# The experts dealt to the fourteen blocks of a mixture anew, and one one-hot written a quarter earlier

## The chip, the cores and the metric

The kernel runs on one core of a Trainium2 chip. A core has a matrix engine (TensorE; PE in the profile, with PEld for the loading of its stationary operand), three engines for elementwise work (VectorE, DVE; ScalarE, ACT; GpSimd, POOL), and SyncE (SP), which issues the loads from the chip's memory here. The metric is the device time of one execution in microseconds (us): the median of several runs, lower is better.

## The reference

A two-layer encoder over 512 tokens of width 1024. Each layer adds a mixer (windowed attention beside a short convolution, and one output projection) and then a mixture of experts to the stream; a final norm ends it. The change touches the mixture alone:

```python
group_logits = (xf @ w_rg).astype(jnp.float32) + b_rg.astype(jnp.float32)
grp = jnp.argmax(group_logits, axis=-1)              # one of 4 groups
...
top_logit, top_local = lax.top_k(in_group, TOP_K)    # 2 of its 8 experts
gates = p_grp * jax.nn.softmax(top_logit, axis=-1)
...
def expert_block(args):
    xb, e = args
    return (jax.nn.silu(xb @ w_gate[e]) * (xb @ w_up[e])) @ w_down[e]
```

Each of the 512 tokens goes to two of 32 experts. An expert has w_gate and w_up of 1024 x 512 and w_down of 512 x 1024, all float32: 6.3 MB, and all 32 of them are read in each layer.

## The kernel before

**Slots and blocks.** The router ranks the experts of a layer by how many tokens they got. The ranks below STATIC (0 to 3) are given to experts 0 to 3 whatever their counts, so that their weights can be loaded before the router has decided; the others go by size, rank 4 the largest. The table BLOCKS (lines 39 to 54) is fixed when the kernel is built: a block is 128 rows of TensorE's output, and its entries (rank, slots) say which ranks share the rows and how many slots each gets. The slots of a rank, 128, 96, 64 or 32, are the same wherever it stands. RANK, BASE, SLOTS, OFF and FIRST are worked out from the table, and the routing (order, route) takes its constants from them. What does not fit goes through spill, a loop that runs as often as the counts need.

**One block**, function block(b, between). Gate and up: in four quarters (kq) of the 1024 inputs, first gate and then up, for each expert of the block two matmul calls per piece of rows into the PSUM buffers "A". A piece is as wide as the smallest step that fits the block's slots (w in the code: 128, 64 or 32 rows), and the pieces of a block stand side by side in the array. Then Silu on ACT and a product on DVE, four transposes ("B"), and down in four quarters c into "C"; last, the result is split into a high and a low part (yhi, ylo) for the sum. The functions in `between` run after quarter 0, 1, 2 or 3 of gate and up, or at "a" and "t" between gate/up and down.

**What runs in between.** For the next group of blocks (GROUPS pairs them: (0,1), (2), (3,4), (5,6), ...): onehot(j) writes the 0/1 matrix of tokens by slots, eight DVE instructions on a 128 x 256 tile each and one small one on POOL; rows_of and slots look up each slot's token and gate; gather multiplies the tokens by the one-hot into the block's inputs. For the block before: combine adds its result into x, with a PSUM pair "D", "F" and an add on DVE for each half of a tile (line 1282). In block 2 all_parts splits the stream x into a high part (ACT, line 1175) and a low part (DVE, line 1176) once for all later gathers; the gathers before that use x itself. SUMS lets block 4 add two blocks' results and block 5 two more.

**Loads.** load() lists every weight tile in the order of use (the list todo): for each block by quarter, gate before up, expert by expert, and then the down tiles. A tile is 512 KB. An expert has twelve: four gate, four up, four down. pump() issues the next loads on SP's queue as long as fewer than N4 - keep tiles are held (N4 = 42 buffers in the pool t4); done() gives a tile back after its last matmul and pumps again. The rest of the pool serves hidden inputs, one-hots, the parts of x and the blocks' results; mem["keep"] is set by stage (20 for blocks 3 and 4, then 15, and 21 in the last block but one). SP runs its loads in the order of the program, and each waits there until the buffer that it was given is free. The weights of ranks 4 and up are fetched with the expert's number in a register, so only after order().

**Order of the engines.** In the blocks TensorE's instructions are kept in program order (pin(T)), each behind the instruction before it on its engine. The instructions of DVE, ACT and POOL are placed by a planner at build time. At block 8 a register is loaded on all engines (the count for spill) between two blocks.

Of the kernel before, what the change touches and what calls it, by code (L numbers as in the profile page):

```python
# [40 lines left out]
    [(2, 64), (3, 64)],  # L41
    [(19, 32), (20, 32), (21, 32), (22, 32)],
    [(8, 64), (9, 64)],
    [(4, 128)],
    [(10, 64), (11, 64)],
    [(5, 96), (23, 32)],
    [(12, 64), (13, 64)],
    [(6, 96), (24, 32)],
    [(14, 64), (15, 64)],
    [(7, 96), (25, 32)],  # L50
    [(18, 64), (26, 32), (27, 32)],
    [(28, 32), (29, 32), (30, 32), (31, 32)],
    [(16, 64), (17, 64)],
]
NBLK = len(BLOCKS)
RANK, BASE, SLOTS, OFF, FIRST = [], [], [], [], []
# [122 lines left out]
def trunk(ctx, tc, x_d, norm_mix, w_in, attn_sink, conv_w, norm_attn_out, norm_conv_out, w_out,  # L179
# [10 lines left out]
    def t4(shape, dt=F32):  # L190
        return t4p.tile(list(shape), dt, name="t4", tag="t4")

    def t2(shape, dt=F32):
        return t2p.tile(list(shape), dt, name="t2", tag="t2")

    def ps(tag, shape=(P, 512)):
        return psp.tile(list(shape), F32, name=tag, tag=tag, bufs=1 if tag in "DF" else 2)

    def small(name, shape, dt=F32, bufs=1):
        return smp.tile(list(shape), dt, name=name, tag=name, bufs=bufs)  # L200

    def f(ap):
        return ap.bitcast(F32)
# [138 lines left out]
    def pin(*engines):  # L342
        for e in (V, A, T, GP):
            e.pinned = e in engines
# [655 lines left out]
    def past(q):  # L1000

        ab, sc = q["ab"], q["sc"]

        cn = ps("B", (P, 4))
        a0 = _cols["rank"][0]
        for t in range(NT):
            T.matmul(cn[:E, 0:1], ab[:, t], onesb[:, 0:1], start=t == 0, stop=t == NT - 1)
        T.matmul(cn[:E, 1:2], q["mt"], cst[:E, a0 + 2:a0 + 3], start=True, stop=True)
        V.tensor_copy(sc[:, 3:4], cn[:E, 1:2])
        V.tensor_tensor(sc[:, 2:3], cn[:E, 0:1], sc[:, 3:4], op=OP.subtract)  # L1010
        V.tensor_scalar(sc[:, 5:6], sc[:, 2:3], 0.0, None, op0=OP.is_gt)
        for b in range(1, 4):
            V.tensor_scalar(sc[:, 6:7], sc[:, 2:3], float(P * b), None, op0=OP.is_gt)
            V.tensor_tensor(sc[:, 5:6], sc[:, 5:6], sc[:, 6:7], op=OP.add)
        nbb = t2([E, P])
        V.tensor_copy(nbb, sc[:, 5:6].to_broadcast([E, P]))
        return nbb

    def places(q, nbb):

        v, oh1, oh2, wk = (q[n] for n in ("v", "oh1", "oh2", "wk"))

        def col(n):
            return v[:, n, :]

        bp = ps("B", (P, E + 1))
        T.matmul(bp, nbb, C("below")[:E], start=True, stop=True)
        bs = small("bs", [P, E + 1])
        V.tensor_copy(bs, bp)

        rb_ = small("rowso", [P, E])
        V.scalar_tensor_tensor(rb_, bs[:, :E], float(P), q["rows"][:, 0], op0=OP.mult, op1=OP.subtract)
        V.tensor_scalar(rb_, rb_, 1.0, None, op0=OP.add)
        ov = q["me"]
        V.tensor_tensor(ov, q["rks"], rb_[:, None, :].to_broadcast([P, NT, E]), op=OP.add)
        V.tensor_tensor(ov, ov, q["ge"], op=OP.mult)
        for n, oh in ((0, oh1), (1, oh2)):
            V.tensor_tensor(wk, oh, ov, op=OP.mult)
            V.tensor_reduce(col(20 + n), wk, axis=AX.X, op=OP.add)
            V.tensor_scalar(col(20 + n), col(20 + n), -1.0, None, op0=OP.add)  # L1040

        eb = t4([1, MAXB, E])
        V.tensor_tensor(eb, bs[0:1, None, 1:E + 1].to_broadcast([1, MAXB, E]),
                        iota[0:1, :MAXB, None].to_broadcast([1, MAXB, E]), op=OP.is_le)
        et = small("et", [1, MAXB])
        V.tensor_reduce(et, eb, axis=AX.X, op=OP.add)
        V.tensor_scalar(et, et, float(E - 1), None, op0=OP.min)
        ni = small("ni", [1, 4], I32)
        V.tensor_copy(ni[:, 0:1], bs[0:1, E:E + 1])
        return et, ni  # L1050
# [89 lines left out]
    def moe(l, before):  # L1140
# [4 lines left out]
        def onehot(j):  # L1145

            b, w = GROUPS[j][0], len(GROUPS[j]) * P
            sq = small("sq", [P, 2, NT], bufs=2)
            GP.tensor_scalar(sq, q["v"][:, 16:18, :], -float(b * P), None, op0=OP.add)  # L1149
            oh = t4([P, NT, 2 * P], F32R)  # L1150
            io = iota[:, :w]
            for t in range(NT):
                V.tensor_scalar(oh[:, t, :w], io, sq[:, 0, t:t + 1], None, op0=OP.is_equal)
                V.scalar_tensor_tensor(oh[:, t, :w], io, sq[:, 1, t:t + 1], f(oh[:, t, :w]), op0=OP.is_equal, op1=OP.add)  # L1154
            ohq[j] = oh
# [51 lines left out]
        def rows_of(j):  # L1207
            w = len(GROUPS[j]) * P
            p = ps("B", (P, 2 * P))
            for t in range(NT):  # L1210
                T.matmul(p[:NROW, :w], st["tab"][:, t], ohq[j][:, t, :w], start=t == 0, stop=t == NT - 1)
            st["rows"] = t2([NROW, 2 * P])
            A.activation(st["rows"][:, :w], p[:NROW, :w], AF.Copy)
# [61 lines left out]
        def combine(b, t, tags="DF"):  # L1275
            yhi, ylo, gm = yy[b]
            for n in range(2):
                s = slice(n * 512, (n + 1) * 512)
                p = ps(tags[n])
                T.matmul(p, gm[:, t * P:(t + 1) * P], yhi[:, s], start=True, stop=False)  # L1280
                T.matmul(p, gm[:, t * P:(t + 1) * P], ylo[:, s], start=False, stop=True)
                V.tensor_add(x[:, t, s], x[:, t, s], p)  # L1282
# [3 lines left out]
        def begin(t):  # L1286

            sums[t] = [ps(tag) for tag in BANKS[l][t]]
            for n in range(2):
                T.matmul(sums[t][n], ident, x[:, t, n * 512:(n + 1) * 512], start=True, stop=False)  # L1290
# [32 lines left out]
        def both(*what):  # L1323
            return lambda: [fn() for fn in what]
# [6 lines left out]
        for b in range(NBLK):  # L1331
            if b == 5:
                nbb = past(q)
            if b == 6:
                et, ni = places(q, nbb)
            if b == 8:
                over = et, nc.values_load(
                    ni[0:1, 0:1], min_val=0, max_val=MAXB,
                    skip_runtime_bounds_check_because="an expert's slots are 32 at least: fewer blocks than experts")

            late = SUMS.get(b, [b - 1])
            c = [lambda t=t: [combine(n, t) for n in late] for t in range(NT)]
            j = GROUP_OF[b] + 1
            if b == 0:
                mem["experts"] = True
                btw = {0: lambda: order(l, q), 1: rest, 3: first, "a": lambda: gather1(1, 4, ND)}
            elif b == 1:
                mem["keep"] = KEEP_SECOND
                btw = {1: lambda: onehot(1), "a": both(lambda: rows_of(1), lambda: gather1(2, 0, 4)),
                       "t": both(lambda: slots(1), lambda: gather1(2, 4, ND))}  # L1350
            elif b == 2:
                ga = [lambda k=k: gather(j, k) for k in range(0, ND, 2)]
                btw = {1: lambda: onehot(j), 2: all_parts, "a": both(lambda: rows_of(j), ga[0], ga[1]),
                       "t": both(ga[2], lambda: slots(j), ga[3])}
            elif b == NBLK - 1:
                mem["keep"] = KEEP_MOE
                btw = {0: both(c[0], c[1]), 1: both(c[2], c[3]), "a": lambda: spill(l, q, *over),
                       "t": lambda: [begin(t) for t in range(AHEAD[l])]}
                if not overflow:
                    del btw["a"]  # L1360
            elif b % 2:
                mem["keep"] = KEEP_LATE if b == 3 else KEEP_MOE
                ga = [lambda k=k: gather(j, k) for k in (0, 2)]
                btw = {1: lambda: onehot(j), "a": both(c[0], ga[0], c[1]), "t": both(c[2], ga[1], c[3])}
            else:
                ga = [lambda k=k: gather(j, k) for k in (4, 6)]
                btw = {"a": both(lambda: rows_of(j), c[0], ga[0], c[1]), "t": both(c[2], lambda: slots(j), ga[1], c[3])}
            pin(*((T,) if b < PIN_MOE else ()))
            if b == NBLK - 2:
                mem["keep"] = KEEP_MOE + 6  # L1370
            block(b, btw)
# [9 lines left out]
    for l in range(DEPTH):  # L1381
        before = moe(l, before)
# [44 lines left out]
```

## Time and profile before

| | us |
|---|---|
| median of 3 runs | 1406.32 (1406.25 to 1407.89) |
| the profiled execution | 1408.32 |
| its span, first to last instruction | 1406.5 |
| PE busy in the span | 1340.6 (95%) |
| PEld busy | 774.8 (55%) |
| DVE busy | 608.9 (43%) |
| ACT busy | 374.0 (27%) |
| POOL busy | 118.8 (8%) |

TensorE's granted clock is 0.993 of full speed over the span. The loads move 439.61 MB, 313 GB/s on the mean. Lines with L175 are those of a helper through which the engines' calls go, so the tile names say what an instruction is: A gate and up, C down, B gathers and transposes, D and F the adds of a block's result. Experts run in layer 0 from about 231 to 704 us and in layer 1 from about 924 to 1400 us. A matmul on float32 shows as two rows, and the matmuls of pieces that stand side by side overlap. Loads are counted from 1 within a layer where the text numbers them, blocks from 0.

### The profile page before, as it was taken

How to read it: one execution, taken by the hardware profiler on the slowest of the kernel's cores; microseconds unless marked ns; L12 is line 12 of the kernel's file. 1: busy time of each engine (PE TensorE's matmuls, PEld its weight loads, DVE VectorE, ACT ScalarE, POOL GpSimd, SP SyncE). 2: the span in 40 equal slices, each digit the busy share in tenths (PEclk: the TensorE clock that was granted, in tenths of full speed). 3: DMA queues.
4: the chain of work that ended last, by engine and by line, in shares of the span. 5: the costliest groups of instructions: out<-in, count | busy, mean ns of one | idle time of the engine just before them, and what ended most of it. 6: DMA issues, size and time to landing. Idle time of an engine off the chain costs nothing. (4 is left out here: it accounts for less than half of the span.)

```text
span 1406.5 us, 21931 instructions
## 1 busy us (share of the span) xinstructions
PE 1340.6 (95%) x7783; PEld 774.8 (55%) x7783; DVE 608.9 (43%) x1483; ACT 374.0 (27%) x816; POOL 118.8 (8%) x130
## 2 busy tenths in 40 slices
PE   5999999999999999999989999999899999999997
PEld 5888786545544444433368887864445444454143
DVE  4788845222344322322267888341333443324032
ACT  4556631221101111101155656221211011111002
POOL 2101440000000000000030015200000000000000
PEclk9999999999999999999999999999999999999999
DMA  8521368999989999999971224789999899999995
GB/s 266 169 74 62 114 247 305 348 378 418 403 329 357 418 413 419 419 418 420 361 240 45 76 75 136 263 335 352 397 419 363 314 418 409 418 419 419 419 419 229
DMA packets 161106, 439.61 MB, mean 313 GB/s; under 512 B 19368, under 2 KB 56416, under 8 KB 160992
## 3 DMA queue, kind: packets, MB, share of 16 engines
q1 hardware_dynamic: 160992, 438.16, 80.6%
q8 instruction: 63, 1.03, 0.3%
q14 instruction: 51, 0.42, 0.1%
HBM read 436.00 MB, written 2.10 MB: 311 GB/s over the span
## 5 line engine op out<-in xcount | busy, mean ns | idle before, releaser
L175 PE MATMUL A<-t,t 128*32 128x512 f32 (+3 forms) x3724 | 720.7, 527 | 13.9 <-DMA t<-in_w_expert_up_dram 4.0
L175 PEld LDWEIGHTS A<-t,t 128*32 128x32 f32 (+2 forms) x3724 | 343.5, 145 | 344.2 <-issue 240.0
L175 PE MATMUL C<-t,t 128*32 128x512 f32 (+4 forms) x1384 | 232.1, 567 | 3.0 <-ACT t L1256 1.5
L175 PEld LDWEIGHTS C<-t,t 128*32 128x32 f32 (+2 forms) x1384 | 84.5, 128 | 134.8 <-issue 112.9
L396 DVE SCALAR_TENSOR_TENSOR t<-C,tg,t 128x512 fp32r<-128x512 f32 x56 | 41.5, 749 | 204.4 <-ACT t L395 202.6
L175 PE MATMUL B<-t,t 128*128 128x256 f32 (+3 forms) x836 | 115.0, 289 | 7.4 <-DVE t L1176 4.9
L175 PEld LDWEIGHTS B<-t,t 128*128 128x128 f32 (+1 forms) x836 | 106.7, 191 | 23.1 <-DVE t L1176 7.8
L1251 DVE SCALAR_TENSOR_TENSOR t<-A,tg,t 128x512 f32<-128x512 f32 x28 | 21.0, 750 | 222.3 <-PE A L175 206.4
L175 PE MATMUL D<-t,t 128*128 128x512 f32 (+1 forms) x374 | 99.7, 365 | 9.9 <-DVE x L1282 6.4
L1282 DVE TENSOR_TENSOR x<-x,D 128x512 f32<-128x512 f32 x104 | 71.3, 685 | 83.9 <-PE D L175 83.5
L1250 ACT ACTIVATE t<-A,tg 128x512 f32<-128x512 f32 x28 | 19.2, 687 | 311.2 <-PE A L175 289.3
L395 ACT ACTIVATE t<-C,tg 128x512 fp32r<-128x512 f32 x56 | 37.8, 687 | 205.5 <-PE C L175 205.2
L175 POOL TENSOR_TENSOR t<-t,t 128x512 f32<-128x512 f32 (+1 forms) x34 | 63.8, 1881 | 236.2 <-PE A L175 124.3
L175 PE MATMUL B<-cst,t 128*128 128x128 f32 (+1 forms) x396 | 61.6, 284 | 21.7 <-DVE t L175 18.0
L1191 ACT ACTIVATE t<-B,gf 128x256 f32<-128x256 f32 (+1 forms) x96 | 38.3, 454 | 146.2 <-PE B L175 136.5
L175 PEld LDWEIGHTS D<-t,t 128*128 128x128 f32 x374 | 53.3, 177 | 40.6 <-issue 13.2
L1282 DVE TENSOR_TENSOR x<-x,F 128x512 f32<-128x512 f32 x104 | 70.8, 680 | 7.5 <-PE F L175 7.5
L175 PE MATMUL F<-t,t 128*128 128x512 f32 x214 | 72.0, 416 | 0.2
L175 PEld LDWEIGHTS B<-cst,t 128*128 128x128 f32 (+1 forms) x396 | 50.4, 154 | 34.7 <-issue 12.7
L175 PEld LDWEIGHTS F<-t,t 128*128 128x128 f32 x214 | 36.7, 188 | 23.1 <-DVE x L1282 14.2
L392 ACT ACTIVATE t<-t 128x1024 fp32r<-128x1024 f32 x44 | 46.1, 1058 | 0.2
L1149 POOL TENSOR_SCALAR sq<-rv 128x8 f32<-128x8 f32 x16 | 3.9, 248 | 492.0 <-DVE t L1154 456.9
(250 smaller groups left out, 1033.4 us busy)
## 6 DMA issues: line engine op xcount, KB each, us to landing
t<-in_w_expert_gate_dram SPq DMA_DIRECT2D x256, 512.0 KB, 9.8
t<-in_w_expert_up_dram SPq DMA_DIRECT2D x256, 512.0 KB, 9.3
t<-in_w_expert_down_dram SPq DMA_DIRECT2D x256, 512.0 KB, 9.8
t<-in_w_in_dram SPq DMA_DIRECT2D x36, 512.0 KB, 6.1
t<-in_w_out_dram SPq DMA_DIRECT2D x16, 512.0 KB, 3.8
x<-in_x_dram SPq DMA_DIRECT2D x4, 512.0 KB
out_dram<-t SPq DMA_DIRECT2D x3, 512.0 KB, 2.6
t<-in_norm_mix_dram SPq DMA_DIRECT2D x2, 512.0 KB
```

The costliest lines, as they stand in the source:

```text
L175: return (lambda *args, **kw: self.tc.keep_in_program_order(fn(*args, **kw))) if self.pinned else fn
L392: A.activation(hi, src, AF.Copy)
L395: A.activation(hi, src, AF.Copy, scale=scale)
L396: V.scalar_tensor_tensor(lo, src, scale, f(hi), op0=OP.mult, op1=OP.subtract)
L1149: GP.tensor_scalar(sq, q["v"][:, 16:18, :], -float(b * P), None, op0=OP.add)
L1191: A.activation(hg[b][c // 4][:, c % 4 + cc, :w], p[:, cc, :w], AF.Copy, scale=g_ffn[:, c + cc:c + cc + 1])
L1250: A.activation(a, pg, AF.Silu, scale=rs)
L1251: V.scalar_tensor_tensor(a, pu, rs, a, op0=OP.mult, op1=OP.mult)
L1282: V.tensor_add(x[:, t, s], x[:, t, s], p)
```

## The change

The table keeps every rank and its slots and deals them to the blocks anew from the block numbered 4 on. Before, the blocks held 2, 2, 4, 2, 1, 2, 2, 2, 2, 2, 2, 3, 4 and 2 experts; after, 2, 2, 4, 2, 2, 3, 2, 3, 1, 2, 2, 2, 2 and 3. The one block with a single expert (rank 4, 128 slots) is the ninth instead of the fifth, and there is one four-expert block, the third, instead of two. Since the list of loads follows the table, the weights come in the new order. Of the fourteen blocks seven instead of six have pieces of 32 rows, and six instead of seven pieces of 64.

The second part moves onehot(j) of the third block (b == 2), which writes the one-hot for blocks 3 and 4, from behind the second quarter of gate and up to behind the first.

```diff
     [(2, 64), (3, 64)],
     [(19, 32), (20, 32), (21, 32), (22, 32)],
     [(8, 64), (9, 64)],
+    [(5, 96), (29, 32)],
+    [(16, 64), (23, 32), (24, 32)],
+    [(10, 64), (11, 64)],
+    [(17, 64), (25, 32), (26, 32)],
     [(4, 128)],
-    [(10, 64), (11, 64)],
-    [(5, 96), (23, 32)],
+    [(6, 96), (30, 32)],
     [(12, 64), (13, 64)],
-    [(6, 96), (24, 32)],
+    [(7, 96), (31, 32)],
     [(14, 64), (15, 64)],
-    [(7, 96), (25, 32)],
-    [(18, 64), (26, 32), (27, 32)],
-    [(28, 32), (29, 32), (30, 32), (31, 32)],
-    [(16, 64), (17, 64)],
+    [(18, 64), (27, 32), (28, 32)],
 ]
...
             elif b == 2:
                 ga = [lambda k=k: gather(j, k) for k in range(0, ND, 2)]
-                btw = {1: lambda: onehot(j), 2: all_parts, "a": both(lambda: rows_of(j), ga[0], ga[1]),
+                btw = {0: lambda: onehot(j), 2: all_parts, "a": both(lambda: rows_of(j), ga[0], ga[1]),
                        "t": both(ga[2], lambda: slots(j), ga[3])}
```

## The prediction, made before the changed kernel ran

> **What bounds the kernel now.** I read the page's slices first, then the timeline of TensorE's own row (PE) through one layer's experts, then the busy time by stretch, one stretch per block, and last the queue of SP.
>
> ```profile
> span 1406.5 us, 21931 instructions
> ...
> DMA  8521368999989999999971224789999899999995
> ```
>
> The two runs of 9 are the two layers' experts: the transfers are full there, and PE looks full too. The PE timeline at block 12 of layer 0, of four experts, shows which one is late. Columns: start, length, then the instructions; what ended an idle gap stands in brackets.
>
> ```profile
> 613.70 6.87 PE L175 MATMUL A<-t,t 128*32 128x512 f32 x50
> 620.75 1.04 PE L175 MATMUL A<-t,t 128*32 128x512 f32 x2 [0.19 <-DMA t<-in_w_expert_up_dram]
> ...
> 643.57 1.90 PE L175 MATMUL A<-t,t 128*32 128x512 f32 x10 [0.19 <-DMA t<-in_w_expert_up_dram]
> ...
> 654.08 4.49 PE L175 MATMUL C<-t,t 128*32 128x512 f32 x38
> ...
> 663.78 1.90 PE L175 MATMUL C<-t,t 128*32 128x512 f32 x10 [0.25 <-DMA t<-in_w_expert_down_dram]
> 665.62 2.94 PE L175 MATMUL A<-t,t 128*64 128x512 f32 x10
> ...
> 670.64 0.73 PE L175 MATMUL D<-t,t 128*128 128x512 f32 x2
> ...
> 692.38 7.09 PE L175 MATMUL C<-t,t 128*64 128x512 f32 x32
> ```
>
> A is gate and up, C is down. Elsewhere the same work takes this long, whatever the widths of the slots:
>
> ```profile
> 330.61 13.96 PE L175 MATMUL A<-t,t 128*64 128x512 f32 x64
> ...
> 359.97 14.00 PE L175 MATMUL A<-t,t 128*128 128x512 f32 x32
> ...
> 432.85 13.94 PE L175 MATMUL A<-t,t 128*32 128x512 f32 x128
> ...
> 456.04 7.07 PE L175 MATMUL C<-t,t 128*32 128x512 f32 x64
> ```
>
> So block 12's A took 613.70 to 645.47, 31.8 us for 13.9: 17.8 lost. Its C took 654.08 to 665.68, 11.6 for 7.1: 4.5 lost. The next block's first quarter took 665.62 to 670.64, 5.0 for a quarter of 13.96 (3.5) and a change of work: 1.4 lost. Together **23.7 us in a layer wait for weights**, though each bracket is small. PE is "busy" there because matmuls that wait between loads count as long rows.
>
> The stretches say why. The columns are PE, PEld, DVE, ACT, POOL busy, PE's granted clock, the transfers' share, GB/s.
>
> ```profile
> 360.00:396.30 36.30, 35.15 (x127) 19.45 (x126) 13.80 (x27) 4.72 (x9) 0.00 (x0) 1.00 0.92 366
> 396.30:432.50 36.20, 34.80 (x171) 16.42 (x170) 16.66 (x38) 3.54 (x7) 0.23 (x1) 1.00 0.84 310
> 432.50:463.00 30.50, 30.50 (x256) 14.29 (x254) 12.81 (x33) 5.26 (x10) 0.00 (x0) 1.00 1.03 418
> 463.00:498.60 35.60, 35.60 (x192) 14.76 (x188) 10.71 (x21) 4.37 (x9) 0.23 (x1) 1.00 1.03 414
> 613.70:665.60 51.90, 47.52 (x254) 15.23 (x246) 7.91 (x16) 4.76 (x10) 0.00 (x0) 1.00 1.03 419
> ```
>
> 419 GB/s is the queue at full pace: a load of 512 KB (524,288 bytes) takes 1.25 us, an expert (12 loads) 15.0. A block of two experts is 30.0 us of queue beside about 30 us of PE, as 432.50:463.00 shows: a balance. Block 4 has one expert, 15 us of queue beside 36.3 of PE. The buffers fill, and the queue stands still: (419 - 366)/419 x 36.3 = 4.6 us in this stretch, (419 - 310)/419 x 36.2 = 9.4 in the next, **14.0 together**. That time is missing at the four-expert block, which asks for 60 us of queue at once. Layer 1 repeats it:
>
> ```profile
> 1053.00:1089.50 36.50, 35.36 (x131) 19.62 (x130) 14.03 (x27) 4.87 (x10) 0.00 (x0) 1.00 0.93 366
> 1089.50:1125.80 36.30, 34.90 (x168) 16.52 (x168) 16.42 (x38) 3.60 (x8) 0.23 (x1) 1.00 0.84 316
> 1306.70:1358.50 51.80, 48.06 (x255) 15.34 (x247) 7.96 (x16) 4.76 (x10) 0.00 (x0) 1.00 1.03 419
> ```
>
> Lost there by the same sum: 4.6 + 8.9 = 13.5 us of queue; the block's 51.8 us stand beside 51.9, so again some 23.6 of PE.
>
> **The change, part by part.**
>
> *Order of the experts.* Nothing is computed less, the bytes are the same, and each block's A and C keep their 14 and 7 us by the rows above. Experts asked for by the end of blocks 4 to 13, before: 11, 13, 15, 17, 19, 21, 23, 26, 30, 32; after: 12, 15, 17, 20, 21, 23, 25, 27, 29, 32. The four-expert peak and its 23.7 us go; what is late next are the three-expert blocks 5, 7 and 13. I set each against the queue, taken as pause-free. The anchor is SP's timeline and the time from issue to landing between 600 and 700 us:
>
> ```profile
> 373.96 17.59 SPq L274 DMA_DIRECT2D t<-in_w_expert_down_dram  x8
> 676.29 8.21 SPq L274 DMA_DIRECT2D t<-in_w_expert_down_dram  x7
> DMA to landing us min/median/max: 9.8/9.9/10.3
> ```
>
> The eight are block 5's down loads, numbers 149 to 156 of the layer (13 experts x 12), so load 149 lands at 373.96 + 9.9 = 383.9 and load n at 383.9 + 1.25 (n - 149).
> - Block 5: its last gate/up load is number 168, at 407.7. PE starts its last eighth at 396.6 + 7/8 x 13.94 = 408.8. It holds by 1.1 us: no wait.
> - Block 7: load 228, at 482.7; PE would start its last eighth at 463.0 + 12.2 = 475.2. **A wait of 7.5 us.** Behind the waiting matmul in PE's queue stand the rest of block 7's A, the adds of block 6 and its C; DVE and ACT idle with it, and their work is not late for anything else.
> - Block 8 takes 15 us of queue beside some 30 of PE, so the queue is 15 us further ahead after it; from there two experts a block are the balance.
> - Block 13: PE comes to it at 665.6 - 22.3 + 7.5 = 650.8 and asks for its last gate/up load, number 372, no sooner than 12.2 later, at 663.0; it lands at 662.7. Its last down load lands at 677.7 and is asked for at 692.4 - 23.7 + 7.5 + 5.3 = 681.5. No wait.
>
> Two ends for layer 0 follow. **By PE**: 692.38 + 7.09 = 699.5, less 23.7, plus 7.5: 683.3. **By the queue**: the last load was issued by 676.29 + 8.21 = 684.5 and landed by 694.4; with the 14.0 us of standing still gone it lands at 680.4, and C's last quarter takes 1.8: 682.2.
>
> Which of them decides hangs on a piece of PE's order. In block 7 PE runs part of block 8's A between adds:
>
> ```profile
> 480.43 1.06 PE L175 MATMUL A<-t,t 128*32 128x512 f32 x6
> ...
> 482.51 1.90 PE L175 MATMUL A<-t,t 128*32 128x512 f32 x10
> ...
> 485.01 1.06 PE L175 MATMUL A<-t,t 128*32 128x512 f32 x6
> ...
> 489.05 1.92 PE L175 MATMUL A<-t,t 128*32 128x512 f32 x14
> ...
> 498.58 10.49 PE L175 MATMUL A<-t,t 128*32 128x512 f32 x92
> ```
>
> Cut up like this it takes 16.4 us for 13.9: 2.5 lost. In the new order block 8's first load is number 241, landing at 498.9, after all of block 7's; an order made from what is ready would not put it ahead. I take it as gone: PE's end is 680.8, and the queue's 682.2 decides. Gain in layer 0: 699.5 - 682.2 = 17.3. Layer 1, by its own rows:
>
> ```profile
> 1367.90 9.11 SPq L274 DMA_DIRECT2D t<-in_w_expert_down_dram  x8
> 1386.49 7.09 PE L175 MATMUL C<-t,t 128*64 128x512 f32 x32
> ```
>
> The last load landed by 1377.0 + 9.9 = 1386.9, less 13.5, plus 1.8: 1375.2 for 1393.6, a gain of 18.4. **Sum: 35.7 us.** Bounds for the terms: the wait gone whole, 2 x 23.6 = 47; PE's end with the cut-up kept, 2 x 16.2 = 32.
>
> One rule speaks against a queue at 419: the Trainium skill, "DMA: Bandwidth & Descriptors", section "Where 436 GB/s comes from", says that for transfers from HBM a limit near 358 GB/s per core binds. This trace disagrees, with 418 and 419 in its full stretches.
>
> *One-hot a quarter earlier.* Its eight DVE instructions and one on POOL stay; it issues no DMA and passes no other instruction on POOL, but takes one buffer of the loads' pool one quarter (3.5 us) sooner.
>
> ```profile
> 301.43 1.14 DVE L1153 TENSOR_SCALAR t<-cst,sq 128x256 fp32r<-128x256 f32 x4 [5.62 <-PE A L175]
> 304.85 1.21 ACT L1175 ACTIVATE t<-x 128x1024 fp32r<-128x1024 f32 x1 [9.82 <-PE A L175]
> L175 PE MATMUL B<-t,t 128*128 128x256 f32 x640 | 88.1, 291 | 7.4 <-DVE t L1176 4.9 <-DVE tg L1227 1.5 <-ACT t L1191 1.0
> ```
>
> DVE had waited for PE (for a buffer), so the one-hot moves to about 298. What PE waits for afterwards, 4.9 us over both layers, are the splits of L1176, and these start from ACT, which waits for PE's third quarter and not for DVE. I count 0; its bounds are a gain of 4.9, and a loss of one load held back a quarter, 3.5 a layer. Even a gain in PE at block 2 is eaten by a longer wait at block 7 while the queue decides. DVE has 5.6 us of idle time there, which is its cover.
>
> Own time: the profiled run took 1408.3 us, 1.8 outside its span of 1406.5, so 1372.6 after; the median of the runs is 2.0 below the profiled one: 1406.3 - 35.7 = **1370.6 us**.
>
> **The rivals.**
> 1. *PE never starves* (the queue gains time early, or block 7 finds its weights): 23.6 a layer, 1359. For it: block 5 misses by little. Against it: load 228 would have to land 7.5 us earlier than a full queue can. 0.10.
> 2. *The cut-up stays and waits.* PE takes its instructions in order: at 3.5 us behind A's end (487.9) it would wait for load 241 until 498.9, 11.0 us, with block 7's C behind it, and keep the cut-up's 2.5: 683.3 + 11.0 leaves 5.2 of gain a layer, 1396. Against it: the load order. 0.08.
> 3. *Loads wait for a certain buffer.* Of what SP waited for between 377 and 424 us (in all, times, longest), the first is
>
> ```profile
> SPq L274 <- PE F L175: 12.1, 3, 10.4
> ```
>
> F are the adds of a block's result: the longest pause ended with these, not with weights used up. SP issues in order, so one such load holds all. One pause of 10.4 in each layer leaves 6.9 and 8.0: 1391, 0.10. **The slower side**: two of them in a layer, at blocks 5 and 7, are 20.8 us, 3.5 and 2.4 beyond the gains: 1412. It decides from 17.3 us of standing still a layer. Against it: such a pause came with a pool that was full, and these blocks empty it faster. Slower 0.04, about the same 0.03.
> 4. *A queue without pauses runs slower.* From 1.32 us a load (17.3 us over the 235 loads after number 149; 396 GB/s) on nothing is left. For it: no stretch here is 300 us without a pause at 419. Against it: 414 to 419 in four of the rows above. At 396 the time is unchanged, and below it grows by about 3 us a layer (235 loads of 1.3) for each 1%. 0.01, within the slower side. By the 358 GB/s that the Trainium skill gives ("DMA: Bandwidth & Descriptors"), the last load would land at 727 by estimate and the time be about 1465.
>
> **How the numbers follow.** The forecast, 1364 to 1377, has 0.64; the cases of 1, 2 and 3 have 0.10, 0.08 and 0.10. About 0.2% (2.8 us) is what a measurement here tells from no change. Faster 0.92, same 0.03, slower 0.05. The range, 1360 to 1393, holds the forecast, most of case 1 and the single pause, 0.8 in all.
>
> **What would show it.** Right: the two low stretches (366, 310) read near 419, PE's A takes 14 us in blocks 11 and 12 and some 21 in block 7, and C of block 13 ends near 682. Wrong: a wait for weights in block 13, queue pauses anywhere after 330, or gate matmuls of block 8 standing in block 7. Wrong in the sum: an end at 676 (PE alone) or past 690.

## The result, and the profile after

| | before | after |
|---|---|---|
| median of 5 runs each, us | 1406.32 (1405.72 to 1407.89) | 1374.05 (1373.07 to 1375.33) |
| ratio, 95% interval | | 0.9768 (0.9755 to 0.9782) |
| the profiled execution, us | 1408.32 | 1374.31 |
| its span, us | 1406.5 | 1372.5 |

The kernel is faster by 2.3%, 32.3 us by the medians and 34.0 between the two profiled executions. The forecast was 1370.6, its range 1360 to 1393.

The page's first line and its slices of the transfers, after:

```profile
span 1372.5 us, 22313 instructions
...
DMA  8522276899999999999891224688999999999996
```

Each layer's row of 9 has no 8 in its middle any more. The busy time by stretch shows the same without rounding (columns: PE, PEld, DVE, ACT, POOL busy, PE's granted clock, the transfers' share, GB/s). The stretches are blocks 4, 5, 7 (with the start of what follows it), 8 to 11, 12 and 13 of layer 0:

```profile
358.24:394.60 36.36, 35.23 (x270) 16.45 (x269) 13.74 (x26) 4.59 (x9) 0.00 (x0) 1.00 1.03 419
394.60:431.20 36.60, 35.16 (x272) 16.10 (x267) 16.64 (x38) 3.85 (x9) 0.23 (x1) 1.00 1.03 419
...
461.40:500.40 39.00, 37.38 (x247) 13.96 (x245) 10.32 (x20) 3.66 (x7) 0.23 (x1) 1.00 1.03 419
500.40:619.00 118.60, 118.60 (x756) 57.74 (x752) 36.63 (x76) 18.26 (x35) 0.00 (x0) 1.00 1.03 419
619.00:648.60 29.60, 29.60 (x160) 14.04 (x156) 8.11 (x17) 4.20 (x10) 0.00 (x0) 1.00 1.03 419
648.60:683.20 34.60, 32.19 (x223) 10.45 (x221) 8.01 (x14) 2.67 (x4) 0.00 (x0) 1.00 0.93 372
```

The stretches that read 366 and 310 GB/s before now read 419, and so do all others up to 648.6. The last reads less because the loads run out before it ends.

The timeline of PE shows where the weights are late now. Columns as before: start, length, instructions, and in brackets what ended an idle gap.

```profile
461.43 6.59 PE L175 MATMUL A<-t,t 128*32 128x512 f32 x54
468.19 2.29 PE L175 MATMUL A<-t,t 128*32 128x512 f32 x14 [0.17 <-DMA t<-in_w_expert_up_dram]
...
483.08 1.90 PE L175 MATMUL A<-t,t 128*32 128x512 f32 x10 [0.20 <-DMA t<-in_w_expert_up_dram]
484.91 0.73 PE L175 MATMUL D<-t,t 128*128 128x512 f32 x2
...
493.38 7.07 PE L175 MATMUL C<-t,t 128*32 128x512 f32 x64
...
619.02 13.95 PE L175 MATMUL A<-t,t 128*64 128x512 f32 x64
...
673.94 7.21 PE L175 MATMUL C<-t,t 128*32 128x512 f32 x54
681.33 1.90 PE L175 MATMUL C<-t,t 128*32 128x512 f32 x10 [0.18 <-SPq L1061]
```

Block 7's A took 461.43 to 484.98, 23.55 us for 13.94: a wait of 9.6. Block 12's A, 31.8 us long when it had four experts, is back at 13.95. Block 13's C ran from 673.94 to 683.23, 9.29 for 7.07: some 2.2 us of waiting for the last down tiles. Nothing else from block 2 on waits for weights, so 23.7 us of waiting became 9.6 + 2.2 = 11.8. The rest of the gain is block 8's A, which now runs in one piece (2.5), and PE reaching block 3 earlier (1.7, of which 1.5 is the clock of this one execution, below).

The last loads of both layers on SP's timeline, each with the time from issue to landing of those twelve loads, and C of block 13 in layer 1:

```profile
656.42 14.70 SPq L274 DMA_DIRECT2D t<-in_w_expert_down_dram  x12
...
DMA to landing us min/median/max: 10.5/10.5/10.5
```
```profile
1333.38 14.06 SPq L274 DMA_DIRECT2D t<-in_w_expert_down_dram  x12
...
DMA to landing us min/median/max: 9.9/9.9/9.9
```
```profile
1352.50 7.08 PE L175 MATMUL C<-t,t 128*32 128x512 f32 x64
```

A run of twelve on SP ends with the last issue, which itself is 0.33 long: the last loads went out at 670.8 and 1347.1. With 10.5 and 9.9 us to landing they were there at 681.3 and 1357.0. C ended at 683.2 in layer 0, 16.2 earlier than before (699.5), and at 1359.6 in layer 1, 34.0 earlier than before (1393.6).

### The profile page after: what moved, and what is told of

Its sections match the earlier page's. It is cut to its first block, busy times and chain, and to the rows that moved or that the text cites. A ratio compares the mean times of both kernels' runs of the same rounds, so it can differ in the third digit from the quotient of the medians.

```text
span 1372.5 us, 22313 instructions
## 1 busy us (share of the span) xinstructions
PE 1311.0 (96%) x7975; PEld 768.2 (56%) x7975; DVE 607.8 (44%) x1483; ACT 374.3 (27%) x816; POOL 119.0 (9%) x130
## 5 line engine op out<-in xcount | busy, mean ns | idle before, releaser
L175 PE MATMUL A<-t,t 128*32 128x512 f32 (+3 forms) x3852 | 698.6, 529 | 9.8 <-DVE t L396 2.3
L175 PEld LDWEIGHTS A<-t,t 128*32 128x32 f32 (+2 forms) x3852 | 339.6, 143 | 326.7 <-issue 238.2
L175 PE MATMUL C<-t,t 128*32 128x512 f32 (+4 forms) x1448 | 226.7, 568 | 1.7 <-ACT t L1256 1.5
L175 PEld LDWEIGHTS B<-cst,t 128*128 128x128 f32 (+1 forms) x396 | 49.8, 153 | 36.4 <-issue 16.3
```

The source lines that it names most:

```text
L175: return (lambda *args, **kw: self.tc.keep_in_program_order(fn(*args, **kw))) if self.pinned else fn
```

## The theory and its rivals

**Two ends.** A layer's experts end at the later of two times: PE's own end (the sum of its work and of its waits at blocks that ask for more weights than have landed), or the landing of the last load and the little that PE still does with it. The change brings both forward, and they now lie within 1 or 2 us of each other: in layer 0 the queue's end is 2.2 us later than PE's own (681.0), in layer 1 PE's is 0.8 later (the last quarter of C is asked for at 1352.50 + 5.3 = 1357.8, and the weights were there at 1357.0).

The rivals: the queue alone decides, so that any load less is time won; PE's wait at block 7 alone decides; and the one-hot, not the order, brings a part of the gain. Six kernels tell these apart. Since executions start up to some 3 us apart, lengths within layer 0 are counted below from the start of block 2's A (294.20 in both before and after) to the end of block 13's C: **405.3 before, 389.0 after**.

## Experiment 1 and 2: each part of the change alone

The new order with the one-hot at its old place:

```diff
-                btw = {0: lambda: onehot(j), 2: all_parts, "a": both(lambda: rows_of(j), ga[0], ga[1]),
+                btw = {1: lambda: onehot(j), 2: all_parts, "a": both(lambda: rows_of(j), ga[0], ga[1]),
```

> The new deal of experts with the one-hot left behind the second quarter. Theory of two ends (a layer's experts end at the later of PE's own end and the last load): PE comes 1.7 us later to block 3 in each layer and waits 1.7 us less at block 7, whose loads land at the same time; 1374 us, within 1.5. Rival, that the 1.7 us won behind block 2 arrive at the end: 1374.0 + 3.4 = 1377.5.

The old table with the one-hot at the first quarter:

```diff
-                btw = {1: lambda: onehot(j), 2: all_parts, "a": both(lambda: rows_of(j), ga[0], ga[1]),
+                btw = {0: lambda: onehot(j), 2: all_parts, "a": both(lambda: rows_of(j), ga[0], ga[1]),
```

> The old deal with the one-hot behind the first quarter. Theory of two ends: PE is 1.7 us earlier in each layer up to block 11 and loses it in the wait for the four experts of block 12; 1406 us, within 1.5. Rival, that the time won arrives at the end: 1403.

The order alone took 1374.66 us (1373.25 to 1377.14), 0.9769 (0.9756 to 0.9783) of the time before; the one-hot alone 1407.48 (1405.25 to 1408.62), 1.0000 (0.9991 to 1.0009). The gain is the order's.

On DVE's timeline of after the one-hot starts when the prediction said:

```profile
298.01 1.14 DVE L1153 TENSOR_SCALAR t<-cst,sq 128x256 fp32r<-128x256 f32 x4 [2.19 <-PE A L175]
```

In the profiled execution of after PE also comes to block 3 earlier, 34.7 us after block 2's start (328.88 - 294.20) instead of 36.4 (330.61 - 294.20). That looks like the one-hot's work, but it isn't. Nearly all of it lies in one gather behind the splits, 25 matmul rows that took 4.75 us before and 3.25 after:

```profile
312.55 4.75 PE L175 MATMUL B<-t,t 128*128 128x256 f32 x25 [0.64 <-DVE t L1176]
...
330.61 1.94 PE L175 MATMUL A<-t,t 128*64 128x512 f32 x8
```
```profile
312.49 3.25 PE L175 MATMUL B<-t,t 128*128 128x256 f32 x25 [0.63 <-DVE t L1176]
...
328.88 3.65 PE L175 MATMUL A<-t,t 128*64 128x512 f32 x16
```

The stretches inside that gather, of before, of after and of experiment 3's kernel, which has the early one-hot too and took 4.75 us as well, show what differs. It is PE's granted clock, the third number from the right:

```profile
312.60:317.10 4.50, 4.50 (x25) 4.50 (x26) 0.00 (x0) 0.84 (x2) 0.00 (x0) 0.63 1.02 419
...
312.60:315.50 2.90, 2.90 (x25) 2.90 (x26) 0.00 (x0) 0.84 (x2) 0.00 (x0) 1.00 1.03 422
...
311.20:315.70 4.50, 4.50 (x26) 4.50 (x27) 0.00 (x0) 0.84 (x2) 0.00 (x0) 0.63 1.03 421
```

Over both layers of the eight profiled kernels this gather took 3.25 or 3.26 us at a clock of 1.00 (four times), 4.49 to 4.75 at 0.61 to 0.67 (ten times) and 5.70 at 0.50 (twice), and with either place of the one-hot there are fast ones and slow ones. Without the gather the way from block 2's start to block 3's takes 31.5 to 31.7 us with the one-hot at its old place and 31.4 to 31.6 at the new one. So the one-hot itself is worth some 0.1 us in a layer, and the early start of layer 0 belongs to that one execution; in its layer 1 the gather took 4.75 again.

The early start is gone again four blocks later. In the order's own run the gather took 4.75, PE came to block 3 after 36.3 us, and block 7 started later:

```profile
462.52 8.43 PE L175 MATMUL A<-t,t 128*32 128x512 f32 x70
...
482.33 1.90 PE L175 MATMUL A<-t,t 128*32 128x512 f32 x10 [0.20 <-DMA t<-in_w_expert_up_dram]
```

Its A took 462.52 to 484.23, 21.7: a wait of 7.8 instead of 9.6. From block 2's start the layer took 388.9 us, as against 389.0 after. PE that comes earlier waits longer for the same load.

In the old order it was not so. The one profiled execution of the one-hot alone had the gather at full clock in layer 0 (3.26) and not in layer 1 (4.67); layer 0 was 1.6 us shorter than before and layer 1 was not. What was expected of this run, that block 12's wait eats such a lead, didn't come: block 12's A took 31.8 us as before. The queue went ahead with PE instead, its two low stretches read 377 and 314 GB/s instead of 366 and 310, and its last load went out 2.0 us earlier counted from block 2's start. So where the queue stands still until PE frees buffers, time that PE wins ahead of that place can reach the end; one execution shows it. The medians show no gain, 1407.48 against 1407.44 in the 21 runs of before beside it, as the one-hot itself wins next to nothing.

## Experiment 3: the three-expert block behind the single one

Blocks 7 and 8 of after are exchanged, so that the queue has a block of 15 us to run ahead before three experts are asked for.

```diff
-    [(17, 64), (25, 32), (26, 32)],
     [(4, 128)],
+    [(17, 64), (25, 32), (26, 32)],
```

> The changed kernel with blocks 7 (three experts) and 8 (one) exchanged. All theories: block 8's weights are there by then, so PE's waits at block 7 (9.6 us in layer 0, 8.3 in layer 1) go. Two ends: the queue has the same loads and stays without a pause, the last load of layer 0 lands near 680.7 again and the waits come back in block 13; 1372 to 1375 us. Rival, PE alone (a wait of PE that goes shortens the layer): 1374.0 - 17.9 = 1356. A third, that the single-expert block makes the queue pause again: a stretch below 400 GB/s and 1377 or more.

It took 1373.24 us (1371.95 to 1374.66), 0.9759 (0.9746 to 0.9772), which the runs can't tell from after. The timeline of PE in that kernel:

```profile
461.57 14.00 PE L175 MATMUL A<-t,t 128*128 128x512 f32 x32
...
478.33 1.06 PE L175 MATMUL A<-t,t 128*32 128x512 f32 x6
...
654.34 5.40 PE L175 MATMUL A<-t,t 128*32 128x512 f32 x38
...
664.41 1.90 PE L175 MATMUL A<-t,t 128*32 128x512 f32 x10 [0.93 <-DMA t<-in_w_expert_up_dram]
...
671.82 6.72 PE L175 MATMUL C<-t,t 128*32 128x512 f32 x52
...
679.95 1.90 PE L175 MATMUL C<-t,t 128*32 128x512 f32 x10 [0.19 <-SPq L1061]
```

Block 7 no longer waits. But the second half of block 13's A took 654.34 to 666.31, 12.0 instead of 7.1, and its C 671.82 to 681.85, 10.0 instead of 7.1: 7.8 us of waiting stand there now. The last load went out at 669.4 and landed 10.5 us later, at 679.9, and C ended 1.9 behind it, as in after. The wait of block 7 was hidden behind the queue's end all along. That PE's wait alone decides has fallen.

The row at 478.33 also answers a question of the prediction. With the weights of the following block there in time, pieces of its A stand between the adds again (the cut-up); in after, where they come later, they don't. Why the planner does so was not looked into.

## Experiment 4: a queue without pauses, and nothing else

The old deal, with the last four-expert block and the single one exchanged in place: the four small experts come fifth, where the buffers had been full, and the single one thirteenth.

```diff
-    [(4, 128)],
+    [(28, 32), (29, 32), (30, 32), (31, 32)],
     [(10, 64), (11, 64)],
...
     [(18, 64), (26, 32), (27, 32)],
-    [(28, 32), (29, 32), (30, 32), (31, 32)],
+    [(4, 128)],
     [(16, 64), (17, 64)],
```

> The old deal with two blocks exchanged: the four-expert block (ranks 28 to 31) stands fifth and the single one (rank 4) thirteenth. All: the queue has no pause, its low stretches are gone, the last load lands near 680. Two ends: PE waits some 15 us in block 4 and a few more in blocks 5 and 11, and comes to block 13 as late as before; 1396 to 1406 us. Rival, the queue alone decides (its pauses were the loss): 1374.

It took 1406.54 us (1404.09 to 1408.31), 0.9995 (0.9985 to 1.0004). Its busy time by stretch, and its PE timeline:

```profile
329.00:389.50 60.50, 57.09 (x297) 19.57 (x290) 11.70 (x22) 6.29 (x11) 0.23 (x1) 1.00 1.03 419
389.50:429.90 40.40, 38.38 (x211) 17.90 (x211) 17.67 (x44) 4.72 (x9) 0.23 (x1) 1.00 1.03 419
...
601.00:622.00 21.00, 19.90 (x137) 4.94 (x126) 3.53 (x11) 1.75 (x3) 0.00 (x0) 1.00 1.03 419
622.00:671.00 49.00, 49.00 (x241) 26.89 (x241) 15.37 (x28) 7.30 (x16) 0.00 (x0) 1.00 1.03 418
```
```profile
360.08 6.51 PE L175 MATMUL A<-t,t 128*32 128x512 f32 x54
...
387.55 1.90 PE L175 MATMUL A<-t,t 128*32 128x512 f32 x10 [0.20 <-DMA t<-in_w_expert_up_dram]
...
412.24 10.09 PE L175 MATMUL A<-t,t 128*64 128x512 f32 x42
...
427.96 1.93 PE L175 MATMUL A<-t,t 128*64 128x512 f32 x6 [0.22 <-DMA t<-in_w_expert_up_dram]
...
601.27 9.66 PE L175 MATMUL A<-t,t 128*32 128x512 f32 x84
...
619.88 1.90 PE L175 MATMUL A<-t,t 128*32 128x512 f32 x10 [0.20 <-DMA t<-in_w_expert_up_dram]
```

The queue runs without a pause, and its last load goes out at 671.3, within half a microsecond of after's. Nothing is won by it: A of blocks 4, 5 and 11 took 29.4, 17.7 and 20.5 us for 14.0 each, 25.7 of waiting, a little more than the 23.7 that it replaces; block 8's A runs in one piece here (2.5 less), behind the same block 7 as before, its first load having gone out at 489.6 instead of 458.4. C of block 13 ended at 699.0, 17.9 us after the last weights had landed. That the queue alone decides has fallen: the same bytes at the same pace end 16 us apart with the order.

## Experiment 5 and 6: twelve loads less, in two places

In each a block's last expert computes with the weights of the one before it, and its own twelve loads in each layer are left out. The work of PE stays. For block 7:

```diff
+TWIN = {RANK.index(26): RANK.index(25)}
...
-            os = range(FIRST[blk], FIRST[blk] + len(BLOCKS[blk]))
+            os = [o for o in range(FIRST[blk], FIRST[blk] + len(BLOCKS[blk])) if o not in TWIN]
...
-... live[nm, l, o, kq][:, k],
+... live[nm, l, TWIN.get(o, o), kq][:, k],
...
-                        done((nm, l, o, kq))
+                        if o not in TWIN:
+                            done((nm, l, o, kq))
```

(The same for the down tiles; the helper's line is L177 in these kernels. For block 13 the ranks are 28 and 27.)

> The changed kernel without the twelve loads of block 7's third expert in each layer: its slots are computed with the second expert's weights, so this part of the result is another expert's, and PE's work is the same. Two ends: the queue ends 15 us earlier a layer, PE's waits at block 7 (9.6 and 8.3 us) go and PE decides: layer 0 ends near 671.4 instead of 683.2, layer 1 gains 8 to 9 of its own; 1352 to 1356 us. Rival, the queue alone: 30 us less, 1344. Rival, the long matmuls of block 7 are no wait for weights: 1374.

> The changed kernel without the twelve loads of block 13's second expert (rank 27 keeps its own, rank 28 is computed with rank 27's weights, which this leaves out of the result). Two ends: the last load lands 15 us earlier, but the waits at block 7 stay and PE decides in both layers: layer 0 ends 2.1 us earlier (the wait in its last down matmuls), layer 1 as before; 1371 to 1374 us. Rival, the queue alone: 1344.

The first took 1355.49 us (1353.34 to 1356.42), 0.9629 (0.9614 to 0.9644), the second 1371.66 (1370.01 to 1372.66), 0.9748 (0.9735 to 0.9761). The same twelve loads are worth 18.6 us at block 7 and 2.4 at block 13 (against after's 1374.05). For block 13 the intervals of the two ratios still touch, so the 2.4 rests on the profiled layers below. The PE timelines of the first and the second:

```profile
462.72 13.94 PE L177 MATMUL A<-t,t 128*32 128x512 f32 x128
...
665.62 7.07 PE L177 MATMUL C<-t,t 128*32 128x512 f32 x64
```
```profile
462.73 8.75 PE L177 MATMUL A<-t,t 128*32 128x512 f32 x70
...
482.86 1.91 PE L177 MATMUL A<-t,t 128*32 128x512 f32 x10 [0.20 <-DMA t<-in_w_expert_up_dram]
...
673.67 7.07 PE L177 MATMUL C<-t,t 128*32 128x512 f32 x64
```

Without the loads of block 7 there is no wait in block 7 and none at the end. From block 2's start layer 0 took 377.2 us, 11.8 less than after: the 9.6 and the 2.2 that were counted as waits. The queue ended 15 us earlier than after's in layer 0, but PE's work then ends the layer.

Without those of block 13 the last load goes out 15.8 us earlier, block 7's wait stays (462.73 to 484.77, 22.0: 8.1), and only the wait in C goes: layer 0 took 386.7 us, 2.3 less than after. Either end alone thus yields a few microseconds before the other takes over; a load less at block 7 moves both.

## Why the prediction was right, point by point

- **The queue's pauses go, and the last load lands at 680.4.** Right within 1 us: every stretch from 358 to 649 is at 419, and the last load landed at 681.3. Of the 0.9 us, 0.6 is the way from issue to landing, 10.5 instead of 9.9. The prediction's other figure for the same load, 677.7 by the anchor with 1.25 us a load, was 3.6 off: from load 149, issued at 373.15, to the last, number 384, it was (670.79 - 373.15)/235 = 1.267 (414 GB/s by the loads' own bytes; the profile doesn't say where the stretches' 419 has the other 1%). The sum by the pauses was the better one.
- **The wait in block 7, 7.5 us.** Right in place and in landing: its last gate/up load was used at 483.1, forecast for 482.7. The wait was 9.6 because PE came 1.6 us earlier (461.43 instead of 463.0), by the clock of one gather. In the order's own run, without that lead, it was 7.8.
- **The one-hot, counted at 0.** Right: some 0.1 us in a layer. The prediction also said that a lead of PE ahead of block 7 would be eaten there, and the lead that the clock gave was.
- **Block 8's A in one piece.** Right (14.00 us from 500.38). The reason given, that the weights would not be there, fits: the third experiment, which has them early, brings the cut-up back, and the fourth, which has them late, loses it.
- **No wait in block 5, none in blocks 11 and 12.** Right: 13.94, 13.94 and 13.95.
- **The queue, not PE, ends layer 0.** Right, with C at 683.2 for 682.2, and the last quarter of C behind the landing took 1.9 for 1.8. "No wait" in block 13 held for A; C waited 2.2 us, as the choice of the queue's end implied. That the choice came out was partly luck: the two ends were forecast 1.4 us apart, and the terms were off by as much (0.9 in the landing, 2.1 in block 7's wait).
- **Layer 1.** The queue's end without layer 0's gain was forecast for 1375.2; 16.2 earlier that is 1359.0, and it was 1359.6. But here PE's own end was 0.8 us behind the queue's and decided, which the prediction didn't have.
- **The sum.** 35.7 was forecast and 34.0 measured between the profiled executions (16.2 of 17.3 in layer 0, 17.8 of 18.4 in layer 1). The other 1.7 between 1370.6 and the median of 1374.05 come from the step from the profiled execution to the median: before's was 2.0 above its median and the forecast took the same for after, whose profiled execution was 0.3 above.
- **Why PE looks busy in block 12.** This reading was wrong, though nothing in the sum rests on it: the matmuls that wait are not longer. In before, one took 593 ns on the mean in the stretch 432.85 to 446.7, without a wait, and 600 in 613.7 to 699.4:

```profile
L175 PE MATMUL A<-t,t 128*32 128x512 f32 x128 | 13.9, 593 | 0.0
...
L175 PE MATMUL A<-t,t 128*32 128x512 f32 x128 | 28.2, 600 | 3.5 <-DMA t<-in_w_expert_up_dram 1.7 <-DMA t<-in_w_expert_gate_dram 1.7
```

The same 128 rows cover 28.2 us instead of 13.9 because the pieces no longer stand side by side: each runs when its own load is there, two rows in 1.04 us, instead of four side by side. A stretch in which PE is busy throughout can thus do less than half of the work that the same length does elsewhere.

Of the rivals, a PE that never starves (1359) would have had to find block 7's weights; the fifth experiment shows that its end is there, at 1355, if twelve loads in each layer are taken away. Loads held back by a certain buffer, and a queue slower than 396 GB/s, didn't appear: no wait of SP for a buffer that PE had to free was longer than 0.7 us between 330 and 684, and 419 was held from 329 to 649. The Trainium skill, "DMA: Bandwidth & Descriptors", section "Where 436 GB/s comes from", says that for transfers from HBM a limit near 358 GB/s per core binds. It doesn't bind this kernel, which runs on one core; no run here has two cores loading at once.

What is left: before 306 us of layer 0 the queue still stands still at times, in both kernels alike. Two stretches of after:

```profile
250.00:270.00 20.00, 18.89 (x111) 9.97 (x112) 4.03 (x13) 5.71 (x11) 0.00 (x0) 1.00 0.77 288
...
290.00:306.00 16.00, 16.00 (x132) 4.82 (x132) 4.23 (x10) 2.52 (x3) 0.23 (x1) 1.00 0.97 354
```

By the same sum as in the prediction these are (419 - 288)/419 x 20 = 6.3 and (419 - 354)/419 x 16 = 2.5 us of queue. Of what SP waited for between 232 and 306 us, the first is a buffer that B, the gathers and transposes, gives back:

```profile
SPq L274 <- PE B L175: 16.1, 4, 8.0
```

Since both ends lie close together in after, a queue that gains here should help only as far as PE's wait at block 7 shrinks with it. That was not tried, and no version that ran is measurably faster than after with all its loads.

## What to carry to other kernels

Where one queue feeds one engine through a pool of buffers, set the running total of what is asked for against the running total of what has landed, block by block, and compute two ends: the engine's with its waits, and the queue's with its pauses. An order that removes the pauses but starves the engine early (experiment 4) or one that spares the engine's wait but not the queue (experiment 3) gains nothing by itself. A wait on such an engine is found by comparing equal work in other places, not by its idle time: block 12's A lost 17.8 us before the change, with gaps of mostly 0.2.

## What was not expected of the hardware

A queue that never pauses held 419 GB/s from 329 to 649 us, beside a PE busy for 99% of that time at a granted clock of 1.00; the prediction had given a slower pace a small chance for want of so long a stretch. The last twelve loads of layer 0 took 10.5 us from issue to landing and those of layer 1 9.9, which put the end of layer 0 0.6 us later. And the same gather of 25 matmul rows, in the same place of the program, ran at a granted clock of 1.00, some 0.63 or 0.50 from one execution and one layer to the next, and took 3.25, some 4.7 or 5.70 us: a difference of 1.5 us between two profiles is not yet the work of the edit between them.
